# Memory of the split operands lent to raw weight tiles, and one float32 path for the first and last expert

## The chip, the cores and the metric

The kernel runs on one core of a Trainium2 chip. The metric is device time in microseconds of one execution. A core has a matrix engine (TensorE, PE in the profile, with its weight loads as PEld), a vector engine (DVE), a scalar engine (ACT), GpSimd (POOL) and SyncE (SP). Here SP issues nearly all transfers from device memory, in its program's order.

## The reference

Two layers of a transformer run over 256 latent tokens and 256 context tokens, 1024 features wide. Each layer has a modulated norm, a mixer of four groups (two convolutions, spatial gating, attention), an output projection, and a channel mixer: a dense SwiGLU in layer 0, and in layer 1 a top-2-of-8 expert SwiGLU, on the latent tokens alone. The last part matters here:

```python
logits = (xt @ router_w).astype(jnp.float32) + router_b.astype(jnp.float32)
top_val, top_idx = lax.top_k(logits, TOP_K)
gates = jax.nn.softmax(top_val, axis=-1)
...
def swiglu(h, w1, w3, w2):
    return (jax.nn.silu(h @ w1) * (h @ w3)) @ w2
```

Each expert has w1 and w3 of 1024 x 3584 and w2 of 3584 x 1024 in float32: 44 MB an expert, 352 MB in all, and every expert is read once. An expert computes only the tokens that chose it. A final norm closes.

## The kernel before

**Weight tiles.** All weights come as tiles of 128 partitions x 2048 float32 (1024 KB), in one fixed order, `plan`. `w_dma` (line 102 issues) takes a free slot, the one that has been free longest, and asks SP for the next tile, as long as a slot is free; `release` gives a slot back when the tile's last reader has been written into the program, and calls `w_dma` again. SP then waits at each issue until the engine that read the slot's old tile has finished. Slots in `kept` are not given back; the test is `o not in kept`, by equality. Most slots are pieces of one large buffer, `FA`; as the first layers end, regions of `FA` that hold nothing any more join the list, so that there are more slots at the end than at the start.

**Two ways to multiply.** In most stages a tile is *split*: by halves (chunks of 1024 columns), ACT copies a chunk to float32r as the high part (line 135), DVE subtracts for the low part (line 136), and PE makes three matmuls of each product (lines 243 to 245, `mm3`). High and low parts stand in a ring of slots in the buffer `RA`: four slots (`wbuf`, from column 9728), and a fifth at columns 4096 to 6143 that `w_more` adds when the experts begin. In the other way, *raw*, PE multiplies the tile as it came, in float32, with at most 64 tokens, two halves of the columns side by side on the array (line 1372 for w1 and w3, line 1395 for w2); nothing is split.

**Experts.** After the router the experts are ordered by token count into eight places. Place 0 is always expert 0. Places 1, 3 and 5 (`NAT`) take small experts and always run raw, with room for 64 tokens; places 2, 4 and 6 always run split, with room for 128. Places 0 and 7 have both programs under a branch on the count: split with more than 64 tokens, raw otherwise. Tokens beyond the room go through a loop at the end that is skipped when there are none. In the profiled execution both took the raw program: lines 1372 and 1395 ran 2240 and 560 matmul records, five places of 448 and 112.

A place has seven slices of the hidden width. `up_nat` or `up` multiplies w1 and w3 of a slice (two tiles each), then `lower` multiplies w2 of the slice before (two tiles), then `flip` turns the result: 42 tiles a place, 336 in all. Small steps are hung between the tiles by a list, `agenda`: the gates, `fetch` and `gather` (which pick and modulate the next place's tokens by one-hot matmuls: line 1289 for a raw place, lines 1301, 1306, 1307 and 1310 for a split one), and `scatter` (which adds a place's result to the tokens). While place 6 runs, both gathers for place 7 are hung in, since the branch is still open. Gathered tokens of split places stand in `RA` from column 0, turned slices from column 6144. The order is written out by hand: each engine runs its own part in the program's order.

**Around the first place.** Layer 1's mixer ends with the output projection `w_out` (its four tiles are split). Then come the residual, the router's logits (from slices of `xT`, in `FA` at `oT + 3072`), the ranks, and at line 1579 the load of expert 0's token count, which every engine waits for before it branches; SP too. Transfers of expert tiles begin before that, as slots come free.

Of the kernel before, what the change touches and what calls it, by code (L numbers as in the profile page):

```python
# [34 lines left out]
def tile_hybrid_headgroup_dit_moe(ctx: ExitStack, tc: tile.TileContext, a, out: bass.AP):  # L35
# [8 lines left out]
    RA = cp.tile([P, 17920], F32R, name="RA")  # L44
# [17 lines left out]
    def ra(o, *shape):  # L62
        n = 1
        for s in shape:
            n *= s
        v = RA[:, o:o + n]
        if len(shape) == 2:
            v = v.rearrange("p (a b) -> p a b", a=shape[0])
        return v
# [15 lines left out]
    NW = [4]  # L85
    LESS = [3]
    LIM = [None]
    wbuf = [(ra(W_O + i * 2048, 1024), ra(W_O + i * 2048 + 1024, 1024)) for i in range(4)]
# [22 lines left out]
    kept = []  # L111

# [5 lines left out]
    def w_split(n):  # L118
        while st["split"] < min(n, len(chunks) if LIM[0] is None else LIM[0]):
# [12 lines left out]
            if i >= len(wbuf):  # L132
                wbuf.append(wbuf[i - NW[0]])
            wh, wl = wbuf[i]
# [688 lines left out]
    NAT = (1, 3, 5)  # L823
    RANK = (0, 7, 1, 6, 2, 5, 3, 4)
# [22 lines left out]
    for j, entry in enumerate(plan):  # L847
        if entry[0][0] in ("modr", "mod") or entry[0][0].startswith("moe") and entry[0][1] in NAT:
# [7 lines left out]
    LIM[0] = first_chunk(0)  # L856
    ring = wbuf[0:4]
# [253 lines left out]
    free_slots.append(fa(oM1, 2048))  # L1111

# [5 lines left out]
    HG, HT = 0, 6144  # L1118
# [40 lines left out]
    free_slots.append(fa(oT + 3072, 2048))  # L1159
    for t in range(2):  # L1160
# [113 lines left out]
    gsb = cp.tile([P, NE], F32, name="gsb")  # L1274


    hns = [ybuf[0].rearrange("p (a b) -> p a b", a=8)] + [fa(4096, 8, 64)] * (NE - 1)
    sn = [fa(4096 + 512 + i * 256, 256) for i in range(2)]
# [3 lines left out]
    def gather(e, o, nat=False):  # L1282
        if nat:
            hn = hns[e]
# [8 lines left out]
        h = hg[e] = H(ra(HG + e % 2 * 2048, 8, P), ra(HG + e % 2 * 2048 + 1024, 8, P))  # L1293
# [20 lines left out]
    def slots(e, o_, gcol):  # L1314
# [5 lines left out]
        v = ra(HS + 1024 + (e % 2) * 256, 256)  # L1320
        nc.scalar.copy(v, b[:, 0:256])
        g = gsb[:, e:e + 1]
# [20 lines left out]
    def raw_tile(key):  # L1343
        if key[1] in (0, NE - 1):
            i = st["use"]
            assert i == st["split"]
            j = chunks[i][0]
            for c in range(2):
                if i + c >= len(wbuf):
                    wbuf.append(wbuf[i + c - NW[0]])  # L1350
            st["use"] = st["split"] = i + 2
        else:
            j = raw_j.pop(0)
# [9 lines left out]
    def up_nat(p, i):  # L1363
        b1, b3 = bank(), bank()
        hn = hns[p]
        for w, b in (("moe_w1", b1), ("moe_w3", b3)):
            for r in range(2):
                j, raw = raw_tile((w, p, i))
                for q in range(4):
                    k = 4 * r + q  # L1370
                    for c in range(2):
                        nc.tensor.matmul(b[64 * c:64 * c + 64, 0:256], hn[:, k], raw[:, q, 256 * c:256 * c + 256],  # L1372
                                         start=k == 0, stop=k == 7, skip_group_check=True)
# [3 lines left out]
            if w == "moe_w1":  # L1377
                s = sn[i % 2]
                nc.scalar.activation(s, b1[:, 0:256], AF.Silu)
        nc.vector.tensor_mul(s, s, b3[:, 0:256])  # L1380
        return s

    def flip_nat(g, s):
        b = bank()
        for j in range(2):
            nc.tensor.transpose(b[:, j * P:j * P + P], s[:, j * P:j * P + P], ident)  # L1386
        nc.scalar.copy(hidn[g % 2], b[:, 0:256])  # L1387
        return hidn[g % 2]

    def down_nat(p, i, hid, ya):  # L1390
# [387 lines left out]
```

## Time and profile before

| | |
|---|---|
| median of 3 runs | 1655.82 us (1655.27 to 1655.94) |
| the profiled execution's own time | 1655.85 us |
| its span, first to last instruction | 1654.0 us |
| mean granted TensorE clock | 0.978 |
| PE busy | 1572.3 us, 95% |
| DVE, ACT busy | 935.2 us (57%), 727.8 us (44%) |
| read from device memory | 489.36 MB |

The page gives each engine's busy time over the span and in 40 slices of 41.35 us, the clock the array was granted, and how busy the 16 DMA engines were. Matmul records overlap and their ends are modelled, so that PE's busy share hides short waits: the time that a stretch of known work takes is a better measure than the busy time in it. A table of stretches names for each its bounds and length, then each engine's busy time with the count of instructions, the granted clock, the DMA share and the rate. Everything from about 787 us to 1637 us is the eight expert places.

### The profile page before, as it was taken

Reading aid. Unit: us, or ns where it says so; the run is one execution under the profiler, and the core shown is the slowest. Engines: PE = TensorE matmul, PEld = TensorE weight load, DVE = VectorE, ACT = ScalarE, POOL = GpSimd, SP = SyncE. Lnnn points to the kernel's source line nnn. Section 1 sums busy time; section 2 is a strip of 40 time slices with the busy share of each in tenths; the row PEclk is TensorE's granted clock in tenths of the full one; section 3 lists DMA queues with packets and bytes.
Section 4 is the critical chain, followed back from the end, with each engine's and each line's share of the span. In section 5 each row is a group of like instructions: output and inputs, shape, how many; then the busy total and the mean of one; then the engine's idle time right before and its main releaser. Section 6 shows DMA issues by size and latency. Waiting matters only on the chain. (4 is left out here: it accounts for less than half of the span.)

```text
span 1654.0 us, 23342 instructions
## 1 busy us (share of the span) xinstructions
PE 1572.3 (95%) x8970; PEld 1164.0 (70%) x8970; DVE 935.2 (57%) x1597; ACT 727.8 (44%) x1101; POOL 25.9 (2%) x54
## 2 busy tenths in 40 slices
PE   7999999999999999999998889999999999999995
PEld 5787788888888797887554447875578855678652
DVE  3794578976465799745101038861188811788301
ACT  4447556222224564564211137761277711677201
POOL 0100000000000001000000000000000000000001
PEclk8999899999999999998999999999999999999998
DMA  8635233756584545524899999999999999999895
GB/s 344 234 144 190 107 110 124 271 211 249 180 304 136 187 167 195 187 84 174 359 421 421 421 421 419 422 381 403 421 421 420 377 392 420 421 420 361 333 421 226
DMA packets 69236, 492.14 MB, mean 298 GB/s; under 512 B 7985, under 2 KB 8753, under 8 KB 9713
## 3 DMA queue, kind: packets, MB, share of 16 engines
q1 hardware_dynamic: 67856, 486.97, 74.9%
q0 software_dynamic: 816, 2.72, 0.6%
q8 instruction: 77, 1.26, 0.3%
q10 hardware_dynamic: 432, 0.74, 0.1%
q14 instruction: 55, 0.44, 0.1%
HBM read 489.36 MB, written 1.05 MB: 296 GB/s over the span
## 5 line engine op out<-in xcount | busy, mean ns | idle before, releaser
L136 DVE TENSOR_TENSOR RA<-FA,RA 128x1024 fp32r<-128x1024 f32 x404 | 486.8, 1227 | 151.8 <-ACT RA L135 148.7
L135 ACT CAST RA<-FA 128x1024 fp32r<-128x1024 f32 x404 | 417.5, 1051 | 248.7 <-PE mm L245 146.8
L243 PE MATMUL mm<-RA 128*128 128x512 f32 (+1 forms) x976 | 371.5, 381 | 10.5 <-ACT RA L135 4.4
L244 PE MATMUL mm<-RA 128*128 128x512 f32 (+1 forms) x976 | 365.7, 375 | 3.8 <-DVE RA L136 2.3
L245 PE MATMUL mm<-RA 128*128 128x512 f32 (+1 forms) x976 | 365.0, 374 | 0.0
L243 PEld LDWEIGHTS mm<-RA 128*128 128x128 f32 x976 | 186.0, 191 | 50.0 <-issue 5.8
L1372 PE MATMUL mm<-FA 128*64 128x256 f32 x1792 | 209.4, 385 | 9.2 <-DMA FA<-in_moe_w_dram 7.9
L243 PE MATMUL acc<-RA 128*128 128x512 f32 (+1 forms) x552 | 207.8, 377 | 4.9 <-DVE RA L765 1.8
L244 PEld LDWEIGHTS mm<-RA 128*128 128x128 f32 x976 | 186.4, 191 | 36.1 <-DVE RA L136 3.2
L245 PEld LDWEIGHTS mm<-RA 128*128 128x128 f32 x976 | 186.1, 191 | 32.7
L245 PE MATMUL acc<-RA 128*128 128x512 f32 (+1 forms) x552 | 204.3, 370 | 0.0
L244 PE MATMUL acc<-RA 128*128 128x512 f32 (+1 forms) x552 | 204.2, 370 | 0.0
L1372 PEld LDWEIGHTS mm<-FA 128*64 128x64 f32 x1792 | 126.3, 138 | 79.6 <-issue 12.2
L1395 PE MATMUL acc<-FA 128*64 128x512 f32 x560 | 132.2, 598 | 7.6 <-DMA FA<-in_moe_w_dram 6.3
L243 PEld LDWEIGHTS acc<-RA 128*128 128x128 f32 x552 | 104.5, 189 | 26.2 <-issue 3.4
L245 PEld LDWEIGHTS acc<-RA 128*128 128x128 f32 x552 | 104.4, 189 | 17.9 <-issue 0.3
L244 PEld LDWEIGHTS acc<-RA 128*128 128x128 f32 x552 | 104.5, 189 | 16.2 <-issue 0.2
L1380 DVE TENSOR_TENSOR FA<-FA,mm 128x256 f32<-128x256 f32 x35 | 14.7, 421 | 159.8 <-PE mm L1372 159.8
L310 DVE SCALAR_TENSOR_TENSOR FA<-FA 128x1024 f32<-128x1024 f32 x80 | 94.4, 1221 | 6.5 <-DMA FA<-in_w_modt_dram 6.4
L1395 PEld LDWEIGHTS acc<-FA 128*64 128x64 f32 x560 | 37.5, 136 | 70.2 <-issue 54.4
L1310 DVE TENSOR_TENSOR RA<-lc,RA 128x128 fp32r<-128x128 f32 x32 | 9.3, 290 | 127.1 <-ACT RA L1307 127.1
L1387 ACT COPY FA<-mm 128x256 f32<-128x256 f32 x35 | 13.0, 372 | 142.4 <-PE mm L1386 142.4
(270 smaller groups left out, 1252.8 us busy)
## 6 DMA issues: line engine op xcount, KB each, us to landing
FA<-in_moe_w_dram SPq DMA_DIRECT2D x336, 1024.0 KB, 15.0
FA<-in_w_modt_dram SPq DMA_DIRECT2D x28, 1024.0 KB, 4.9
FA<-in_ffn_dram SPq DMA_DIRECT2D x22, 1024.0 KB, 5.0
FA<-in_ffn_w_dram SPq DMA_DIRECT2D x22, 1024.0 KB, 4.9
FA<-in_w_mod_dram SPq DMA_DIRECT2D x20, 1024.0 KB, 7.0
FA<-in_w_in_dram SPq DMA_DIRECT2D x20, 1024.0 KB, 5.1
FA<-in_w_out_dram SPq DMA_DIRECT2D x12, 1024.0 KB, 4.9
FA<-in_x_dram SPq DMA_DIRECT2D x2, 1024.0 KB, 8.3
```

What stands on the lines that cost most here:

```text
L135: nc.scalar.copy(wh, raw)
L136: nc.vector.tensor_sub(wl, raw, wh)
L243: nc.tensor.matmul(ps, ll, rh, start=start, stop=False, skip_group_check=True)
L244: nc.tensor.matmul(ps, lh, rl, start=False, stop=False, skip_group_check=True)
L245: nc.tensor.matmul(ps, lh, rh, start=False, stop=stop, skip_group_check=True)
L310: nc.vector.scalar_tensor_tensor(o, raw[:, c], 1.0, csb[:, s], op0=OP.mult, op1=OP.mult, accum_out=modT[l][:, 2 * r + c, s:s + 1])
L1310: nc.vector.tensor_sub(h.l[:, k], v["h32"], h.h[:, k])
L1372: nc.tensor.matmul(b[64 * c:64 * c + 64, 0:256], hn[:, k], raw[:, q, 256 * c:256 * c + 256], start=k == 0, stop=k == 7, skip_group_check=True)
L1380: nc.vector.tensor_mul(s, s, b3[:, 0:256])
L1387: nc.scalar.copy(hidn[g % 2], b[:, 0:256])
L1395: nc.tensor.matmul(ya[64 * hf:64 * hf + 64, :], hid[:, jj * P + 64 * r:jj * P + 64 * r + 64], raw[:, 2 * hf + jj], start=i == 0 and r == 0 ...
```

## The change

- `RA` is no longer one buffer but seven (`piece`, R0 to R6), cut at columns 0, 4096, 8192, 9728, 11776, 13824 and 15872. R3 to R6 are the four ring slots. The same memory can be declared again, as float32 for raw tiles or as float32r.
- R1 becomes two more slots for raw tiles, from the time when the last product that reads it (`v`) is written into the program until the end. The fifth ring slot, which lay there, is gone: the ring has four slots throughout.
- `lend` gives pieces out as slots that are used once each. R3 to R6 and R0 (six tiles) are lent when `w_out` has been written; R3 to R6 (four tiles) again in the first slice of places 3 and 5, and before place 7. `take_back` declares them as float32r again: R0 after place 0, R3 to R6 at the end of places 1, 3 and 5.
- `release` tests `kept` by identity, and a call of `w_dma` follows at once where a region of `FA` is added at `oT + 3072`.
- Places 0 and 7 run raw whatever the count. With more than 64 tokens the branch runs each tile's matmuls twice, for two halves of the tokens, with the same weights; with 64 or fewer, the program is the raw one as before. The split gather for place 7 is gone from place 6, and the raw one is spread over place 6 as over the others (`GATH`).
- The gathered tokens of split places have one place in R0 instead of two (only even places use it), and the buffers of the last norm lie elsewhere in `FA`.

```diff
-    RA = cp.tile([P, 17920], F32R, name="RA")
+    def piece(i, dt=F32R):
+        return cp.tile([P, RW[i]], dt, name=f"R{i}", tag=f"R{i}", bufs=1)
+    RO, RW = (0, 4096, 8192, 9728, 11776, 13824, 15872), (4096, 4096, 1536, 2048, 2048, 2048, 2048)
+    RA = [piece(i) for i in range(7)]
...
-    NW = [4]
+    NW = 4
...
     def release(j):
         o = raw_of.pop(j)
-        if o not in kept:
+        if not any(o is x for x in kept):
             free_slots.append(o)
         w_dma()
...
+    def lend(*pieces):
+        for i in pieces:
+            RA[i] = piece(i, F32)
+            for o in range(0, RW[i], 2048):
+                t = RA[i][:, o:o + 2048]
+                lent.append(t)
+                kept.append(t)
+                free_slots.append(t)
+        w_dma()
+
+    def take_back(*pieces):
+        for t in lent:
+            assert not any(t is x for x in list(raw_of.values()) + free_slots)
+        for i in pieces:
+            RA[i] = piece(i)
...
-    def w_more(wh, wl):
-        assert st["split"] >= NW[0] and len(wbuf) == st["split"]
-        wbuf.append((wh, wl))
-        NW[0] += 1
...
-        w_split(i + NW[0] - less - LESS[0])
+        w_split(i + NW - less - LESS[0])
...
     NAT = (1, 3, 5)
+    TWO = (0, NE - 1)
+    RAW = NAT + TWO
...
     for t in range(2):
         nc.scalar.copy(vc[:, t], accs[2 + t])
+    RA[1] = piece(1, F32)
+    free_slots += [RA[1][:, 0:2048], RA[1][:, 2048:4096]]
+    w_dma()
...
     accs = w_out(1, (1, 2, 0, 3), yn1, mid)
     free_slots.append(fa(oM1, 2048))
+    lend(3, 4, 5, 6, 0)
...
     free_slots.append(fa(oT + 3072, 2048))
+    w_dma()
...
+                    for n, hn in enumerate((hns[p], hn_2)[0:1 + two]):
+                        for c in range(2):
+                            nc.tensor.matmul(b[64 * c:64 * c + 64, 256 * n:256 * n + 256], hn[:, k],
+                                             raw[:, q, 256 * c:256 * c + 256], start=k + n == 0, stop=k == 7,
+                                             skip_group_check=True)
...
-    w_more(ra(4096, 1024), ra(5120, 1024))
...
+    def body(g, nat, two=False):
         e, i = divmod(g, NSL)
+        s = up_nat(e, i, two) if nat else up(e, i, hg[e], moe_next)
         if g and g - 1 in hts:
+            lower(g - 1, nat if i else e - 1 in RAW, two)
+            if i == 0 and 1 < e < NE - 1 and nat:
+                lend(3, 4, 5, 6)
+        hts[g] = flip_nat(g, s, two) if nat else flip(g, s)
...
+    either(first_n, first_place)
+    take_back(0)
...
-            if e < NE - 2:
-                plan_late(fetch(e + 1, e + 1 in NAT), GATH)
-            else:
-                plan_late(fetch(e + 1, False), [0] + [9 + 4 * k + d for k in range(KD) for d in (0, 1, 1)])
-                plan_late(fetch(e + 1, True), [45] + [49 + 4 * k + d for k in range(KD) for d in (0, 1, 1)])
+            plan_late(fetch(e + 1, e + 1 in RAW), GATH)
         body(g, e in NAT)
         if e in NAT and i == NSL - 1:
-            w_split(st["use"] + NW[0])
+            take_back(3, 4, 5, 6)
+            w_split(st["use"] + NW)
...
+    lend(3, 4, 5, 6)
+    fg, xg, sq, ss = fa(oM1 + 4096, D), fa(oM1 + 6144, 2, D), fa(oM2 + 3584, 2, D), sm(4)
...
+    either(last_n, last_place)
+    take_back(3, 4, 5, 6)
```

`either` loads the count, writes the program with two halves under the branch's true side and the one with a single half under the other, and asserts that both leave the same lists.

On SP the issues before the first count is loaded stand as follows; `in_moe_w_dram` are expert tiles, FA and R the buffers they land in. Before:

```order
69 L102 DMA FA<-in_w_out_dram 128x2048 x2
70 L102 DMA FA<-in_moe_w_dram 128x2048
71 L102 DMA FA<-in_w_out_dram 128x2048 x2
72 L102 DMA FA<-in_moe_w_dram 128x2048 x8
73 L1579 TENSOR_LOAD ti
```

And with the change (R_5326 is R1, R_5756 to R_5759 are R3 to R6, R_5760 is R0):

```order
70 L108 DMA FA<-in_moe_w_dram 128x2048
71 L108 DMA FA<-in_w_out_dram 128x2048 x2
72 L108 DMA FA<-in_moe_w_dram 128x2048 x2
73 L108 DMA R_5326<-in_moe_w_dram 128x2048 x2
74 L108 DMA FA<-in_moe_w_dram 128x2048 x8
75 L108 DMA R_5756<-in_moe_w_dram 128x2048
76 L108 DMA R_5757<-in_moe_w_dram 128x2048
77 L108 DMA R_5758<-in_moe_w_dram 128x2048
78 L108 DMA R_5759<-in_moe_w_dram 128x2048
79 L108 DMA R_5760<-in_moe_w_dram 128x2048 x2
80 L108 DMA FA<-in_moe_w_dram 128x2048
81 L1603 TENSOR_LOAD ti
```

Nine expert tiles stood ahead of the load of the count, and twenty stand there now. Before, two more followed behind the branch before the first one that needs a tile of place 0 to be used up.

On ACT, in place 6, the split gather (lines 1306 and 1307, once for each of eight blocks of features) stood among the copies of the split. Before:

```order
702 L135 CAST RA<-FA 128x1024 x4
703 L1306 ACTIVATE lc<-mm,modT_75 128x128
704 L1307 ACTIVATE RA<-mm,modT_75 128x128
705 L1442 CAST RA<-mm 128x512
706 L135 CAST RA<-FA 128x1024 x3
707 L1306 ACTIVATE lc<-mm,modT_75 128x128
708 L1307 ACTIVATE RA<-mm,modT_75 128x128
```

With the change the same stretch of place 6 holds the copies (line 159 now, each to one of four ring slots), the raw gather (line 1318), and nothing of a split gather:

```order
829 L159 CAST R_10439<-FA 128x1024
830 L159 CAST R_10436<-R_5326 128x1024
831 L159 CAST R_10437<-R_5326 128x1024
832 L159 CAST R_10438<-R_5326 128x1024
833 L1318 ACTIVATE FA<-mm,modT_81 128x64
834 L1470 CAST R_7311<-mm 128x512
```

The sixteen activations of the split gather, its matmuls on PE and its subtractions on DVE are gone from place 6; some of the copies read their tile from R1.

More of the change, by code (lines that the diff above doesn't have):

```diff
@@ L65, in ra @@
             n *= s
[L66 removed]
+        i = max(i for i in range(7) if RO[i] <= o)
+        assert o + n <= RO[i] + RW[i]
+        v = RA[i][:, o - RO[i]:o - RO[i] + n]
         if len(shape) == 2:
@@ L1312, in gather, with slots @@
         return steps
-    def slots(e, o_, gcol):
+    def slots(e, o_, gcol, part=0):
         b = bank()
@@ L1343, in raw_tile @@
     def raw_tile(key):
[L1344 to L1351, printed above, removed]
-        else:
-            j = raw_j.pop(0)
+        j = raw_j.pop(0)
         assert plan[j][0] == key
@@ L1509, in tile_hybrid_headgroup_dit_moe, with lower @@
     ya = {}
-    def lower(g, nat):
+    def lower(g, nat, two=False):
         e1, i1 = divmod(g, NSL)
         if i1 == 0:
-            ya[e1] = bank("acc") if nat else [bank("acc") for _ in range(2)]
+            ya[e1] = [bank("acc") for _ in range(1 + two if nat else 2)]
         if nat:
@@ L1519, in lower @@
         if i1 == 4:
-            sl[0] = slots(e1, one_hot(e1), list(place(e1))[1])
+            gc = list(place(e1))[1]
+            sl[:] = [slots(e1, one_hot(e1), gc)] + ([slots(e1, oh_2, gc, 1)] if two else [])
         if i1 == NSL - 1 and 0 < e1 < NE - 2:
@@ L1557, in scat_now, with first_place @@
         del agenda[:]
-    def first_place(nat):
-        assert st["use"] == st["split"] == LIM[0] == first_chunk(0)
-        LIM[0] = first_chunk(2)
-        if not nat:
-            first = fetch(0, False)
-            first[0]()
-            w_split(st["use"] + NW[0])
-            hbuf.extend([ybuf[i][:, j * P:j * P + P] for i in range(2) for j in range(2)])
-            run(first[1:])
-            del hbuf[2:]
+    def first_place(two):
+        if two:
+            run(fetch(0, True, 1))
         plan_late(gates(), range(2, 22))
@@ L1571, in first_place @@
         for i in range(NSL):
-            body(i, nat)
-        lower(NSL - 1, nat)
+            body(i, True, two)
+        lower(NSL - 1, True, two)
         for fs in agenda:
@@ L1615, in ends, with last_place @@
         nc.gpsimd.tensor_tensor(xg[:, t, c], xs[:, 2 + t, c], fg[:, c], op=OP.mult)
[L1617 to L1618 removed]
+    def last_place(two):
         scat(NE - 2, False)
[L1620 to L1623 removed]
+        if two:
+            run(fetch(NE - 1, True, 1))
         for i in range(NSL):
[L1625 to L1626 removed]
+            body((NE - 1) * NSL + i, True, two)
+        lower(LAST, True, two)
         nc.gpsimd.dma_start(fg, a["final_g"].to_broadcast([P, D]))
[L1628 to L1637 removed]
+        scat_now(NE - 1, [lambda t=t, hf=hf: ends(t, hf) for hf in range(2) for t in range(2)])
+    either(last_n, last_place)
+    take_back(3, 4, 5, 6)
     raws = [fa(oR, 2048), fa(oR + 2048, 2048)]
@@ L1656, in nxt @@
             raw = raws[(n // 2) % 2][:, c * 1024:c * 1024 + 1024]
-            wh, wl = ring[n % 4]
+            wh, wl = [ra(W_O + n % 4 * 2048 + k * 1024, 1024) for k in range(2)]
             nc.scalar.copy(wh, raw)
```

164 lines of the change are left out of this document (72 added, 92 removed).

## Prediction

> **What bounds the kernel now.** I read the page's slices first, to find the stretch that the change touches.
>
> ```profile
> PE   7999999999999999999998889999999999999995
> DVE  3794578976465799745101038861188811788301
> DMA  8635233756584545524899999999999999999895
> ```
>
> From slice 19 (787 us) on DMA is at 9 nearly throughout: the expert weights. DVE tells the ways apart: near 0 in raw places, 8 in split ones. PE's 9 cannot be trusted for short waits, since matmul ends are modelled. So I cut the trace into stretches of known work:
>
> ```profile
> core 0: us, PE busy (x) PEld busy (x) DVE busy (x) ACT busy (x) POOL busy (x), PEclk, DMA share, GB/s
> 786.70:866.00 79.30, 78.61 (x588) 44.40 (x588) 9.11 (x42) 13.65 (x28) 0.00 (x0) 0.98 0.96 394
> 892.20:973.60 81.40, 71.50 (x494) 36.57 (x490) 4.73 (x14) 10.08 (x26) 0.00 (x0) 1.00 1.01 421
> 973.60:996.20 22.60, 18.24 (x77) 12.21 (x75) 15.05 (x15) 13.14 (x15) 0.00 (x0) 0.92 1.01 421
> 996.20:1104.70 108.50, 108.50 (x501) 88.04 (x498) 95.69 (x91) 83.29 (x93) 0.00 (x0) 1.00 1.01 409
> 1121.60:1192.30 70.70, 70.70 (x502) 37.05 (x498) 9.44 (x21) 11.04 (x28) 0.00 (x0) 1.00 1.01 417
> 1192.30:1212.70 20.40, 18.18 (x77) 12.18 (x75) 14.88 (x15) 13.16 (x15) 0.00 (x0) 0.92 1.01 421
> 1408.90:1429.50 20.60, 16.64 (x74) 10.96 (x75) 15.09 (x16) 13.25 (x16) 0.00 (x0) 1.00 1.02 422
> 1429.50:1549.40 119.90, 118.10 (x557) 96.05 (x555) 99.46 (x102) 88.43 (x109) 0.00 (x0) 1.00 0.97 384
> 1549.40:1611.40 62.00, 61.31 (x466) 34.35 (x467) 7.51 (x14) 5.12 (x13) 0.00 (x0) 1.00 0.96 393
> 1611.40:1636.90 25.50, 20.70 (x122) 8.55 (x122) 0.98 (x3) 1.46 (x4) 0.55 (x1) 1.00 0.83 344
> ```
>
> In order: place 0; most of place 1; the passage into split place 2; its body; place 3, the same stretch as place 1's; the passage into 4; into 6; 6's body up to place 7; place 7 in two parts. Places 1 and 3 do the same products, as the line's own stretches show:
>
> ```profile
> 892.20:973.60 81.40, 42.16 (x354) 24.95 (x350) 1.00 1.01 421
> 1121.60:1192.30 70.70, 41.04 (x354) 23.95 (x350) 1.00 1.01 417
> ```
>
> Line 1372 ran 354 matmuls in both, with the array's clock at 1.00, but place 1 took 10.7 us longer, with DMA at its full 421 GB/s: place 1 waits for its weights, place 3 does not. At that rate a tile of 1024 KB takes 2.49 us. Place 3's stretch uses 354/16 + 12 = 34 tiles, one in 2.08 us, faster than they come; a split body uses 36 in 108.5 us, one in 3.01 us, slower. So the store of loaded tiles grows in split places and shrinks in raw ones, and the first two places are both raw. They start from too little:
>
> ```profile
> L102 SPq DMA_DIRECT2D FA<-in_moe_w_dram x11: 327/328/739, 683.2 to 777.9; - x11
> 786.75 5.52 PE L1372 MATMUL mm<-FA,lc 128*64 128x256 f32 x36 [2.43 <-issue]
> 740.00:760.00 20.00, 20.00 (x128) 15.60 (x127) 12.46 (x43) 11.80 (x23) 0.00 (x0) 1.00 0.71 256
> 760.00:780.00 20.00, 17.96 (x109) 16.50 (x108) 12.08 (x45) 7.73 (x16) 0.59 (x16) 0.81 0.10 28
> ```
>
> Eleven expert tiles have been asked for when place 0's first matmul runs at 786.75. The slots are full, and DMA stands at 0.10 from 760 to 780. The waits on SP say the same:
>
> ```profile
> SPq L102 <- PE mm L1372: 158.8, 91, 11.4
> SPq L1579 <- DVE pv L1493: 19.8, 1, 19.8
> ```
>
> Issues wait for PE to free a slot, and for 19.8 us SP sits at the count with nothing it could have issued.
>
> **The change part by part.** *More tiles at the start.* SP's order has 20 expert tiles ahead of the first use, against 11. The nine: two in R1, one FA slot that the test by identity gives back (before, an equal view in `kept` dropped it), six lent. Do they arrive in time? R1 waits for `v`, whose last matmul ran at 714; R3 to R6 and R0 wait for `w_out`:
>
> ```profile
> L245 PE MATMUL acc<-RA x35: 279/389/498, 713.7 to 765.0; 128*128 128x512 f32 x32, 128*128 128x256 f32 x3
> ```
>
> From 765 to 787 DMA can move 22/2.49 = 8 tiles, more than the seven left. From the first release (a tile is 16 records, of which 36 took 5.52 us) near 790 the stream then runs without a pause. The 62 further tiles up to the last one of place 1's stretch take 62 x 2.49 = 154 us, and the first needs the time of an idle queue:
>
> ```profile
> FA<-in_w_out_dram SPq DMA_DIRECT2D x12, 1024.0 KB, 4.9
> ```
>
> They land by 790 + 154 + 5 = 949. PE needs that one about 12 us before the 973.6 at which it is done now, near 960. So there is a margin of some 11 us, four tiles, and place 1 takes place 3's pace: **10.7 us**. The last tiles of place 0 are late now too; the waits from 860 to 975 name PE's products of w2 as well:
>
> ```profile
> PE mm L1372 <- DMA FA<-in_moe_w_dram: 5.4, 11, 0.8
> PE acc L1395 <- DMA FA<-in_moe_w_dram: 4.6, 8, 1.4
> ```
>
> I take one such wait for place 0, an estimate: **1 us**.
>
> *Passages.* ACT's copies wait there for tiles:
>
> ```profile
> ACT RA L135 <- DMA FA<-in_moe_w_dram: 13.4, 10, 4.7
> ```
>
> PE idles 4.4, 2.2 and 4.0 us in the three passages (22.60 - 18.24, and so on), part of it for the turned slices, which stays. With tiles on chip early I take 3, 1 and 1.5 us: **5.5 us**, between 0 and 10.6.
>
> [...] The passages into 2 and 4 show a clock of 0.92, the one into 6 shows 1.00. [...]
>
> *Place 6 loses the split gather.*
>
> ```profile
> 996.20:1103.90 107.70, 57.78 (x144) 27.02 (x144) 1.00 1.01 411
> 1429.50:1541.00 111.50, 58.56 (x144) 27.07 (x144) 1.00 0.99 392
> 1429.50:1541.00 111.50, 4.24 (x28) 4.20 (x28) 1.00 0.99 392
> ```
>
> The same 144 matmuls of line 243 take 107.7 us in place 2 and 111.5 in place 6; the third row is line 1301 there, absent from place 2. Gain **3.8 us**.
>
> *Place 7.* Its first 32 tiles took 62.0 us, 1.94 each; the last ten 25.5. At 1.94 they take 19.4: **6.1 us**. The cover must grow by three tiles: three permanent slots and four lent ones make seven (17 us), and DMA has room to fill them, since place 6 leaves it at 384 GB/s because slots are full. Places 3 and 5 do not wait now, so their loans are worth nothing alone; they keep the store up when all starts earlier. Over one split and one raw place DMA needs 84 x 2.49 = 209 us and PE 108.5 + 70.7 + 20.4 + 17 (the rest of the raw place, 1104.7 to 1121.6) = 217, so the stream holds.
>
> *A ring of four for five.* This is the cost.
>
> ```profile
> L136 DVE TENSOR_TENSOR RA<-FA,RA 128x1024 fp32r<-128x1024 f32 x258 | 306.9, 1222 | 64.8 <-ACT RA L135 61.9
> L135 ACT CAST RA<-FA 128x1024 fp32r<-128x1024 f32 x258 | 265.2, 1051 | 72.7 <-PE mm L245 36.4 <-PE acc L245 20.7 <-DMA FA<-in_moe_w_dram 13.4
> L243 PE MATMUL mm<-RA 128*128 128x512 f32 x336 | 137.3, 409 | 4.4 <-ACT RA L135 4.4
> L1443 DVE TENSOR_TENSOR RA<-mm,RA 128x512 fp32r<-128x512 f32 x21 | 14.5, 690 | 7.7 <-ACT RA L1442 6.7
> L1432 ACT ACTIVATE lc<-mm 128x512 f32<-128x512 f32 x21 | 12.6, 598 | 5.7 <-PE mm L245 5.6
> ```
>
> ACT waits 57 us for PE to free a ring slot, PE 4.4 us for ACT: the ring is full nearly always. A chunk needs 1.05 + 1.22 = 2.27 us to be split, PE uses one in 107.7/72 = 1.50 us. With four slots, three chunks lie ahead when one is freed, 4.5 us of work against 2.27 and one other operation of ACT or DVE (0.6 to 0.7 us, as in the last two rows). The margin is 1.5 us; only two or three extra operations on top of each other pass it. I take 1 us in all. A bound from above: if each of the 21 split slices lost one 0.7 us operation, 15 us; from below, 0.
>
> *At nothing:* the two-halves branch, since both counts took the other side; declaring pieces again, which issues nothing. The last norm's buffers: its weights load into a slot whose last tile comes just before the final ten, about 19 us ahead of the end, so that these ten hide the load; without that cover it would cost at most its own time:
>
> ```profile
> FA<-in_final_g_dram POOLq DMA_DIRECT2D x1, 512.0 KB, 8.5
> ```
>
> *Sum.* 10.7 + 1 + 5.5 + 3.8 + 6.1 - 1 = 26.1 us. The profiled execution took 1655.85 us (span 1654.0 and 1.85 around it), the median 1655.82, so it stands for the runs. 1655.85 - 26.1 = 1629.7, and since the passages may add the clock and the gather also leaves ACT and DVE, I say **1629 us**.
>
> **Rivals.**
>
> *Half the gain is lost* (the ring costs its 15 us, or lent pieces come late). If no loan helps at all, three permanent slots (7.5 us of stream) remain: place 1 gains 7.5 for 10.7, and 6.1 + 3.8 stay, 17 us in all: 1639. With the ring's 15 us off the full sum it is 1645. Against the late loans: the row of `w_out` ends at 765. For it: the ring's margin is worked out from means.
>
> *The ring of four starves PE: slower.* In places 2, 4 and 6 each freed slot sets ACT, DVE and PE going one after the other. If hand-overs and other work bring that loop over 4 x 1.50 = 6.0 us, it sets the pace; at 7 us a chunk takes 1.75, and 252 chunks lose 63 us: 1629 + 63 = 1692. It turns the whole slower from 6.4 us on (0.107 us for each of 252 chunks, 27 us). Against it: the loop is 2.27 us of splitting, at most 1.50 of matmuls and the hand-overs, under 5.
>
> *The stream stays the bound: same.* If the tiles that come earlier only fill the store earlier, and the whole is set by bytes, nothing is won. Against it: from 790 the 316 remaining tiles need 316 x 2.49 = 787 us, to 1577, and now the last one lands at about 1635. The floor of the stream lies 58 us lower. It would need a rate of 316 x 1.049 MB / 845 us = 392 GB/s to bind as now, and the trace holds 421 for whole places.
>
> [...]
>
> **How the numbers follow.** Prefetch covers place 1 and the end: 0.70, 1621 to 1637 (passages and clock 5 to 8 us better, ring 7 us worse). Half lost, 1637 to 1651: 0.17. Better than 1621: 0.04. Same: 0.04. Ring starves, slower: 0.05. Within 0.2% (3.3 us) a measurement of this kernel cannot tell from no change; faster 0.91, same 0.04, slower 0.05. The range 1618 to 1645 leaves out the last two, the worst of the half, and the little below.
>
> **What would show it.** Right: 20 expert tiles asked for before the first raw matmul; place 1's 34 tiles in about 71 us; no wait of the raw products for DMA in places 1 and 7; a split body of 108 us in all three split places, place 6 no longer apart. Wrong: split bodies above 110 us with PE waiting for line 159 or 160 (the ring); R3 to R6 issued after 787, or SP held at one of them while FA slots are free; DMA under 421 GB/s while PE waits for it.

## The result and the profile after

The changed kernel takes 1626.29 us (median of 4 runs, 1622.73 to 1628.01), the kernel before 1655.55 us beside it (4 runs, 1651.65 to 1655.94). The ratio is 0.983, with a 95% interval of 0.980 to 0.985: some 1.7% less time. The forecast was 1629 us, with 1618 to 1645 as its range.

The profiled execution took 1626.18 us and its span is 1624.4 us, against 1655.85 and 1654.0. The DMA slices of its page:

```profile
DMA  9635323766674545547799999999999999999993
```

DMA's 9s start as they did, but the last slice has a 3: the last weights are there well before the end. The table of stretches of the changed kernel, cut at the same steps of the program as the prediction's table (columns as there):

```profile
core 0: us, PE busy (x) PEld busy (x) DVE busy (x) ACT busy (x) POOL busy (x), PEclk, DMA share, GB/s
786.90:866.10 79.20, 78.69 (x586) 44.54 (x588) 9.12 (x42) 13.67 (x28) 0.00 (x0) 0.98 0.91 369
892.10:959.60 67.50, 67.50 (x495) 36.35 (x492) 4.74 (x14) 10.10 (x26) 0.00 (x0) 1.00 1.01 421
959.60:978.30 18.70, 16.47 (x75) 10.96 (x75) 13.80 (x14) 12.25 (x14) 0.00 (x0) 1.00 1.01 420
978.30:1086.40 108.10, 108.10 (x499) 87.84 (x497) 95.30 (x91) 83.31 (x93) 0.00 (x0) 1.00 1.01 421
1103.30:1174.50 71.20, 71.20 (x507) 37.38 (x504) 9.44 (x21) 11.06 (x28) 0.00 (x0) 1.00 1.01 421
1389.40:1408.10 18.70, 16.47 (x75) 10.96 (x75) 13.71 (x14) 12.27 (x14) 0.00 (x0) 1.00 1.01 422
1408.10:1516.20 108.10, 108.10 (x499) 87.85 (x497) 95.32 (x91) 83.31 (x93) 0.00 (x0) 1.00 1.00 401
1516.20:1525.20 9.00, 6.17 (x29) 4.64 (x27) 3.67 (x4) 1.53 (x2) 0.00 (x0) 1.00 0.98 368
1525.20:1587.20 62.00, 61.46 (x468) 34.60 (x470) 6.94 (x13) 5.12 (x13) 0.55 (x1) 1.00 1.01 420
1587.20:1606.50 19.30, 18.78 (x122) 8.60 (x118) 0.97 (x3) 1.46 (x4) 0.00 (x0) 1.00 0.49 202
1606.50:1624.40 17.90, 1.41 (x10) 0.78 (x8) 6.71 (x20) 4.32 (x10) 4.94 (x4) 0.59 0.16 63
```

In order: place 0; place 1; the passage into place 2; its body; place 3; the passage into 6; the body of place 6; the step into place 7; place 7 in two parts; the end. Each answers to a row of before (the passage into place 4, not shown, takes 18.7 us too):

| stretch | before, us | after, us | gain | predicted |
|---|---|---|---|---|
| place 0 | 79.3 | 79.2 | 0.1 | 1 |
| place 1 | 81.4 | 67.5 | 13.9 | 10.7 |
| passages into 2, 4 and 6 | 22.6, 20.4, 20.6 | 18.7, 18.7, 18.7 | 7.5 | 5.5 |
| body of place 2 | 108.5 | 108.1 | 0.4 | } -1 (ring) |
| place 6 with the step into 7 | 119.9 | 117.1 | 2.8 | } 3.8 (gather) |
| place 7 | 87.5 | 81.3 | 6.2 | 6.1 |
| the end | 17.1 | 17.9 | -0.8 | 0 |
| sum | | | 30.1 | 26.1 |

The spans differ by 29.6; the rest lies in stretches that are not in the table (place 3 takes 71.2 us for 70.7, for example). The lead at the start shows in the issues up to 787 us, by the buffer they land in:

```profile
L108 SPq DMA_DIRECT2D FA<-in_moe_w_dram x12: 327/328/328, 683.6 to 772.6; - x12
L108 SPq DMA_DIRECT2D R<-in_moe_w_dram x8: 328/382/435, 715.1 to 766.6; - x8
```

The first raw product, from the timeline, comes after them all:

```profile
786.88 7.14 PE L1393 MATMUL mm<-FA,lc 128*64 128x256 f32 x48 [1.76 <-issue]
```

Twenty expert tiles are asked for, 8 of them into pieces of the old `RA`, before the first product at 786.88. The waits for expert tiles from 866 us to the end, first before, then with the change:

```profile
ACT RA L135 <- DMA FA<-in_moe_w_dram: 13.4, 10, 4.7
PE mm L1372 <- DMA FA<-in_moe_w_dram: 7.9, 14, 1.3
PE acc L1395 <- DMA FA<-in_moe_w_dram: 6.3, 12, 1.4
```

```profile
ACT R L159 <- DMA FA<-in_moe_w_dram: 1.7, 2, 1.2
```

PE's matmuls wait for none any more, and 0.5 us of ACT's 1.7 lie in the passage into place 2.

### The profile page after: what moved, and what is told of

The parts are those of the page before. It is cut to its first block, busy times and chain, and to the rows that moved or that the text cites. A ratio compares the mean times of both kernels' runs of the same rounds, so it can differ in the third digit from the quotient of the medians.

```text
span 1624.4 us, 23225 instructions
## 1 busy us (share of the span) xinstructions
PE 1562.1 (96%) x8938; PEld 1162.2 (72%) x8938; DVE 932.9 (57%) x1587; ACT 723.1 (45%) x1085; POOL 25.9 (2%) x54
## 5 line engine op out<-in xcount | busy, mean ns | idle before, releaser
L160 DVE TENSOR_TENSOR R<-FA,R 128x1024 fp32r<-128x1024 f32 x368 | 443.9, 1227 | 130.9 <-ACT R L159 127.7
L159 ACT CAST R<-FA 128x1024 fp32r<-128x1024 f32 x368 | 381.4, 1051 | 229.5 <-PE mm L264 131.4
L262 PE MATMUL mm<-R,R 128*128 128x512 f32 (+1 forms) x976 | 369.9, 380 | 10.0 <-ACT R L159 4.4
L263 PE MATMUL mm<-R,R 128*128 128x512 f32 (+1 forms) x976 | 364.7, 374 | 3.5 <-DVE R L160 2.3
L264 PE MATMUL mm<-R,R 128*128 128x512 f32 (+1 forms) x976 | 363.6, 373 | 0.0
L262 PEld LDWEIGHTS mm<-R,R 128*128 128x128 f32 x976 | 185.4, 190 | 48.7 <-ACT R L159 5.1
L262 PE MATMUL acc<-R,R 128*128 128x512 f32 (+1 forms) x552 | 208.2, 378 | 4.9 <-DVE R L784 1.8
L263 PEld LDWEIGHTS mm<-R,R 128*128 128x128 f32 x976 | 185.8, 190 | 35.7 <-DVE R L160 3.2
L264 PEld LDWEIGHTS mm<-R,R 128*128 128x128 f32 x976 | 185.7, 190 | 32.3
L263 PE MATMUL acc<-R,R 128*128 128x512 f32 (+1 forms) x552 | 204.6, 371 | 0.0
L264 PE MATMUL acc<-R,R 128*128 128x512 f32 (+1 forms) x552 | 204.5, 371 | 0.0
L1393 PE MATMUL mm<-FA 128*64 128x256 f32 x1488 | 174.5, 387 | 2.3 <-issue 1.4
L1393 PEld LDWEIGHTS mm<-FA 128*64 128x64 f32 x1488 | 104.8, 138 | 59.5 <-issue 10.4
L262 PEld LDWEIGHTS acc<-R,R 128*128 128x128 f32 x552 | 104.7, 190 | 26.3 <-issue 3.4
L264 PEld LDWEIGHTS acc<-R,R 128*128 128x128 f32 x552 | 104.5, 189 | 17.9 <-issue 0.3
L263 PEld LDWEIGHTS acc<-R,R 128*128 128x128 f32 x552 | 104.7, 190 | 16.5 <-issue 0.3
L1423 PE MATMUL acc<-FA 128*64 128x512 f32 x416 | 96.9, 596 | 1.0 <-ACT FA L1414 1.0
L495 DVE SCALAR_TENSOR_TENSOR FA<-FA,pv 128x512 f32<-128x512 f32 (+1 forms) x128 | 74.1, 612 | 1.2 <-ACT FA L491 0.7
```

Source lines behind the costliest of these rows:

```text
L159: nc.scalar.copy(wh, raw)
L160: nc.vector.tensor_sub(wl, raw, wh)
L262: nc.tensor.matmul(ps, ll, rh, start=start, stop=False, skip_group_check=True)
L263: nc.tensor.matmul(ps, lh, rl, start=False, stop=False, skip_group_check=True)
L264: nc.tensor.matmul(ps, lh, rh, start=False, stop=stop, skip_group_check=True)
L495: nc.vector.scalar_tensor_tensor(acc, src, w, acc, op0=OP.mult, op1=OP.add)
```

## Experiments

Where a few microseconds count, one more number is used beside the medians: the time from the first raw product to the end of the span in the profiled run. What the engines compute before that product is the same in all kernels but one (the transfers ahead of it differ), and yet the product came at anything from 781.70 to 788.94 us (more on this at the end). This time has a spread of its own: the changed kernel's two profiled runs differ by 2.1 us in it.

| kernel | median, us (runs) | ratio to before, 95% | first raw product to end, us |
|---|---|---|---|
| before | 1654.85 to 1655.93 (beside each group) | | 867.3 |
| changed | 1626.29 (4) | 0.9826 [0.9804, 0.9848] | 837.5 |
| changed, again | 1625.51 (5) | 0.9822 [0.9807, 0.9837] | 839.6 |
| no loan at the start | 1637.19 (4) | 0.9881 [0.9865, 0.9898] | 853.7 |
| no later loans | 1625.11 (4) | 0.9812 [0.9796, 0.9828] | 838.7 |
| before, ring of four | 1654.84 (10) | 0.9991 [0.9982, 1.0001] | 871.7 |
| before, one gather | 1653.16 (8) | 0.9980 [0.9967, 0.9994] | 864.8 |
| ring of three | 1639.40 (4) | 0.9919 [0.9896, 0.9943] | 851.8 |
| one slot less | 1628.41 (4) | 0.9849 [0.9828, 0.9871] | 840.4 |
| dense at the scatter | 1626.16 (4) | 0.9830 [0.9807, 0.9854] | 838.4 |
| dense there and in the router | 1627.30 (4) | 0.9841 [0.9819, 0.9862] | 838.6 |
| dense, lent twice | 1625.65 (5) | 0.9816 [0.9797, 0.9835] | 837.4 |
| that, and dense ahead of place 7 | 1630.13 (4) | 0.9849 [0.9833, 0.9865] | 844.1 |

**The loan at the start left out.**

```diff
-    lend(3, 4, 5, 6, 0)
+    w_dma()
```

> The changed kernel without the loan of six tiles (R3 to R6, R0) at the end of the mixer; the later loans and the 14 permanent slots stay. 14 expert tiles instead of 20 are asked for before the first raw matmul. Theory of the lead: in the changed kernel the stream runs without a pause from the first release to the passage into place 2, and the two tiles used there (numbers 88 and 89) are taken the moment they land; so each tile missing at the start costs its 2.49 us, six cost 15 us, and the time is about 1641 us (1638 to 1643). Rival, that the permanent slots carry the gain and the loan only filled slack: place 1 ends with some 4 us of slack in the changed kernel, and no more than 5 us come back, 1627 to 1631.

1637.19 us: 10.9 more than the changed kernel, between the two expectations and nearer to the first. Place 1 and the passage behind it, in this kernel:

```profile
890.60:965.10 74.50, 69.34 (x495) 36.29 (x492) 4.73 (x14) 10.08 (x26) 0.00 (x0) 1.00 1.01 421
965.10:988.10 23.00, 18.22 (x79) 12.25 (x80) 14.63 (x15) 13.44 (x16) 0.00 (x0) 0.97 1.01 421
```

Place 1 takes 74.5 us for 67.5, with the same 495 matmuls, and the passage 23.0 for 18.7. That is the lead at work: six tiles fewer, and the raw places wait again. (The profiled run is the slowest of the four; the medians differ by about what these two stretches show, 7.0 and 4.3 us.) Why 11 us and not the 15 of six tiles? The stretches of place 0, first of the changed kernel, then of this one, show it:

```profile
787.00:800.00 13.00, 12.49 (x98) 8.13 (x100) 2.47 (x13) 4.81 (x6) 0.00 (x0) 0.87 0.63 231
820.00:830.00 10.00, 10.00 (x78) 5.75 (x76) 0.42 (x1) 1.19 (x3) 0.00 (x0) 1.00 0.69 277
```

```profile
787.00:800.00 13.00, 12.48 (x106) 8.28 (x104) 2.47 (x13) 5.96 (x9) 0.00 (x0) 0.92 0.76 299
820.00:830.00 10.00, 10.00 (x72) 5.19 (x70) 0.42 (x1) 1.19 (x3) 0.00 (x0) 1.00 1.01 419
```

From 820 to 830 us the changed kernel's stream runs at 277 GB/s for 419: at 421 GB/s this is 3.4 us given back, of 15. (The 231 for 299 up to 800 us is mostly a matter of when the runs start: this one's first raw product came 1.6 us earlier, and in the same 13 us after it the rate is 248.) The landings in the two traces agree: counted from the first raw product, tile 88, which the passage into place 2 needs, lands at 184.0 us in the changed kernel and at 195.2 here, 11.2 us later and not 15. The loans are used once; when they are spent, the tiles again wait for a permanent slot. (That this pause is a lack of slots is shown below, where the pieces are lent twice.)

**The later loans left out** (the two calls of `lend(3, 4, 5, 6)` behind place 1).

> The changed kernel without the loans in places 3 and 5 and before place 7 (12 tiles in all); the loan at the start stays. Theory of the lead: the three permanent slots are 7.5 us of stream and cover the 6.1 us that place 7 was short; 0 to 2 us lost, 1626 to 1628. Rival, that place 7 lives on the loan: its last ten tiles wait for DMA again, and 5 to 6 us come back, 1631 to 1632.

1625.11 us: they are worth nothing that can be measured. The prediction had said so of those in places 3 and 5; it had counted on the four before place 7, and they too are not needed.

**The kernel before with the ring of four alone.**

```diff
-    w_more(ra(4096, 1024), ra(5120, 1024))
```

> The kernel before with a ring of four slots of split operands instead of five in the expert places; nothing else is changed. Theory: three chunks ahead (4.5 us of PE work) are enough against 2.27 us of splitting and one other operation, so 0 to 1 us, 1655.5 to 1656.5, with split bodies of 108 us. Rival, the ring starves PE: each of 21 split slices loses one operation of 0.7 us, 15 us, 1670, with split bodies of 113 us or more.

The ratio is 0.9991 [0.9982, 1.0001] (the profiled run was the slowest of the ten, hence its 871.7 in the table). The split bodies of places 2, 4 and 6 take 108.5, 108.5 and 111.7 us, for 108.5, 108.5 and 111.5 with five slots. The fifth slot cost nothing to give up.

**The kernel before with a single gather for place 7.** The split gather is moved from place 6 into the split program of place 7, which is not taken here.

> The kernel before with the split gather for place 7 moved out of place 6 and under the branch that is not taken; slots and ring as before. Theory: place 6's body becomes that of places 2 and 4, 108 us for 112, and 3.8 us are won, 1651.7. Rival: place 7 is short of tiles at its end anyway, and a place 6 that ends earlier gives the stream less time to run ahead, so the gain goes into longer waits in place 7 and the time stays at 1655.5.

The median is 2.8 us lower, the interval gives 1.0 to 5.5. The trace shows both theories half right. Body of place 6, the step into place 7, and place 7 in two parts, in this kernel:

```profile
1430.30:1538.40 108.10, 108.10 (x500) 87.94 (x499) 95.14 (x92) 83.32 (x94) 0.00 (x0) 1.00 1.00 410
1538.40:1548.60 10.20, 6.74 (x33) 5.09 (x31) 2.86 (x4) 0.87 (x2) 0.00 (x0) 1.00 0.61 222
1548.60:1610.60 62.00, 61.48 (x454) 34.60 (x456) 6.91 (x12) 5.12 (x13) 0.00 (x0) 0.97 0.95 386
1610.60:1636.90 26.30, 21.98 (x136) 9.27 (x132) 1.00 (x3) 1.46 (x4) 0.55 (x1) 1.00 0.85 352
```

The body takes 108.1 us for the 111.5 of before, as in the changed kernel, and the passage ahead of it 19.1 for 20.6. Then the step into place 7 takes 10.2 for 8.4 and place 7 itself 88.3 for 87.5. The last product ends at 1636.9 in both, but this run's first raw product came at 788.94 us and that of before at 786.75, so that from there the run is 2.2 us ahead, near the 2.8 of the medians. What was lost again lies at the branch, where PE waits 2.06 us for 0.43 (more on this below), and in place 7. The last tile lands at 1634.9 in both, just as the last product needs it, so place 7 still waits for its weights, as the rival had it; but its clock is lower too (0.97 for 1.00), and how much goes to which one trace cannot tell.

**A ring of three** (from the first place on).

```diff
-    NW = 4
+    NW = [4]
...
+    NW[0] = 3
```

> The ring of split operands has three slots instead of four from the first expert on; the fourth stays unused except when it is lent. My account of the ring: when a slot is freed with four slots three chunks lie ahead (4.5 us of matmuls) and splitting takes 2.27 us, so four slots have slack and cost nothing. With three, two chunks (3.0 us) lie ahead of a split of 2.27 us, some 0.4 us of hand-over between the engines, and any one other operation of ACT or DVE (0.6 to 0.7 us) that comes between: the slack is 0.3 us and most slices lose part of such an operation. Expected: split bodies of 110 to 116 us instead of 108.1, so 1632 to 1650. The rival, that PE's pace hides any ring because its matmuls are queued ahead, expects 1625 to 1628 and bodies of 108. The prediction's rival of a starving ring, moved by one slot (a loop of 6 to 7 us over three slots), expects bodies of 150 us or more and 1750.

1639.40 us, 13 more: as the margin said. (The expectation's 0.4 us of hand-over were an estimate; in the changed kernel's body of place 2 DVE starts 0.04 us after the end of the copy that it waits for, at 988.33 us for 988.29.) The passage into place 6 and its body, in this kernel:

```profile
1390.10:1411.60 21.50, 19.27 (x78) 12.82 (x79) 12.99 (x14) 12.08 (x15) 0.00 (x0) 0.92 1.01 421
1411.60:1521.90 110.30, 109.67 (x495) 86.36 (x493) 96.26 (x91) 83.04 (x94) 0.00 (x0) 1.00 0.98 389
```

The body takes 110.3 us for 108.1, the passage 21.5 for 18.7, some of it by the clock (0.92). Place 4 lies between (109.3 and 19.9). With place 2 (108.5 and 20.9) the split places and their passages lose 10.0 us against the changed kernel's first profiled run. Another 2.6 are lost at the step into place 7 (11.6 for 9.0; PE's wait behind the branch is 4.98 us) and 1.7 in place 7 (82.9 for 81.3, its clock 0.97 from 1533.5 to 1596.0 us). The size of the whole agrees with the expectation, its place only in part: I had put all of it into the bodies (110 to 116). The starving ring (1750) is ruled out even for three slots. So the step from five slots to four costs nothing and that from four to three 13 us, of which 10 are seen in the split places.

**One permanent slot less** (the test in `release` drops one `FA` slot again).

> The changed kernel with one permanent slot of the large buffer dropped, as the test by equality dropped it before: 19 tiles instead of 20 ahead of the first use, and 13 permanent slots instead of 14. Taking six early tiles away cost 11 us, 1.8 us a tile. Theory (each tile of the start's lead is worth its share of stream, as far as the margin of 4.3 us at the end of place 1 is used up): the first two tiles lost are covered by the margin, so one tile costs 0 to 1 us: 1626 to 1627.5. Rival (every tile counts alike): 1628 to 1629.

1628.41 us, 2 to 3 more than the changed kernel's two medians. The intervals overlap; the trace decides. Place 1 and the passage into place 2 in this kernel:

```profile
885.40:953.00 67.60, 67.60 (x497) 36.36 (x494) 4.74 (x14) 10.11 (x26) 0.00 (x0) 1.00 1.01 421
953.00:974.00 21.00, 18.12 (x74) 12.07 (x74) 14.02 (x14) 12.29 (x14) 0.00 (x0) 0.92 1.01 420
```

And the longest wait for a weight tile there, from the waits:

```profile
ACT R L159 <- DMA R<-in_moe_w_dram: 3.4, 1, 3.4
```

Place 1 stays at 67.6: its margin was there, as the theory had it. But the passage behind it takes 21.0 for 18.7, with ACT 3.4 us late for a tile and the clock at 0.92. In the changed kernel ACT waits 0.5 us there: the lead is just used up at the second slice of place 2. So a tile less costs about a tile.

**Dense matmuls where the clock falls.** At the end of place 0, PE waits 2.2 us for the scatter's operands, and the granted clock is then 0.60 from 876.8 to 884.0 us. Nine matmuls of ones by ones, into the bank that the scatter's first product overwrites, fill this wait (n is 9 there, and 0 everywhere else):

```diff
                 def product(...):
                     w[0] = bank()
+                    warm(n, w[0])
```

> The changed kernel with nine more matmuls of 128 columns, whose results are thrown away, on PE where it waits 2.2 us at the end of place 0 for the scatter's operands. After that wait the granted clock falls to 0.50 for about 7 us. Theory (the wait lets the clock fall, and filling it keeps the clock): 877 to 884 runs at 1.00, 2 to 3.5 us gained, 1623 to 1624. Rival (the fall comes from something else, or the weights bind at once): no gain, or 0.5 us lost, 1626 to 1627.

Two stretches from there, of the changed kernel and then of this one:

```profile
870.70:874.00 3.30, 1.85 (x10) 0.40 (x6) 0.76 (x1) 0.59 (x1) 0.00 (x0) 1.00 1.01 420
...
876.80:884.00 7.20, 7.14 (x40) 4.18 (x42) 1.60 (x5) 0.39 (x1) 0.00 (x0) 0.60 1.01 419
```

```profile
870.70:874.00 3.30, 3.30 (x23) 2.01 (x20) 0.95 (x2) 0.59 (x1) 0.00 (x0) 1.00 0.99 407
...
876.80:884.00 7.20, 6.75 (x63) 4.48 (x64) 1.39 (x4) 0.38 (x1) 0.00 (x0) 1.00 1.02 424
```

The theory holds at this place: a clock of 1.00 for 0.60, and 63 matmuls for 40 in the same 7.2 us. Place 2's first split product comes 2.4 us earlier after the first raw one (172.1 us for 174.5). Yet the median is 1626.16, no gain. The trace shows tile 88 landing just as ACT asks for it in the passage into place 2 (ACT waits 0.5 us for a tile there), and I took the stream for what gave the gain back.

**The same in the router's stage.** Three such matmuls ahead of each group of the router's transposes, and five ahead of the rank product.

> As the run before, and in the router's stage too: three such matmuls ahead of each of the four groups of transposes, five ahead of the rank matmul. There the clock is 0.50 from 770 to about 791 us, while the matmuls have 8 columns or are few. Theory (a denser array keeps the clock): the gather at 778 to 785 us takes 3.5 us instead of 7, place 0's first products gain 1.5 to 2, the logits 1; the added matmuls cost up to 2 us on PE: 1.5 to 4 us less than the run before, 1619 to 1622. Rival (the dense matmuls are too few to hold the clock, or the wait for the count absorbs the gain): 0 to 2 us slower than the run before.

1627.30 us, no gain: the rival. The stretch of the gather ahead of place 0, in the changed kernel and then in this one:

```profile
778.20:785.10 6.90, 6.90 (x33) 6.73 (x32) 0.68 (x4) 2.83 (x7) 0.25 (x8) 0.50 0.52 209
```

```profile
778.60:782.30 3.70, 3.70 (x34) 3.59 (x33) 0.85 (x5) 2.80 (x7) 0.60 (x16) 1.00 0.71 288
```

And this kernel's first raw product, with the wait ahead of it, from the timeline:

```profile
786.28 7.25 PE L1395 MATMUL mm<-FA,lc 128*64 128x256 f32 x48 [3.95 <-issue]
```

The gather runs at a clock of 1.00 for 0.50 and takes 3.7 us instead of 6.9. PE then waits 3.95 us instead of 1.76, and the first product comes at 786.28 instead of 786.88. The trace has what it waits for: PE's own branch on the count, which lasts 4.37 us here and 3.81 in the changed kernel. It starts while matmuls written before it are still running, 2.3 us before their end in the changed kernel and only 0.7 here. So what the faster gather wins, the branch takes.

**The pieces lent twice.** With the dense matmuls at the scatter, and the six pieces handed out again in place 0 as soon as their tiles are used, four of them again in place 1:

```diff
             body(i, True, two)
+            if i == 2:
+                again(0, 3)
+            if i == 3:
+                again(3, 6)
...
-            if i == 0 and 1 < e < NE - 1 and nat:
+            if i == 0 and 0 < e < NE - 1 and nat:
```

> The dense matmuls at the end of place 0, and the six lent pieces handed out a second time within place 0 (for tiles 33 to 35 and 39 to 41), four of them once more in place 1. The dense matmuls alone won 2.4 us by the clock and gave 1.6 back at the passage into place 2, where tile 88 came late. In the changed kernel DMA pauses for some 3 us between 820 and 830, when the single-use loans are spent. Theory (the stream at tile 88 is the next bound, and the pause is a lack of slots): DMA at full rate from 800 to 890, tile 88 lands 3 us earlier against the first product, and the 2.4 us stay: 1623 to 1624.5, and 2 to 2.4 us less from the first raw product to the place-2 body. Rival (the loss at the passage is not the weights): nothing gained, 1626.

From 820 to 830 us DMA now moves 424 GB/s for 277:

```profile
820.00:830.00 10.00, 10.00 (x76) 5.55 (x74) 0.42 (x1) 1.19 (x3) 0.00 (x0) 1.00 1.02 424
```

So the pause was a lack of slots. Tile 88 lands 3 us earlier against the first product, and no expert tile is waited for in place 1 and the passage behind it. But the median is 1625.65, beside 1625.51 of the changed kernel in the same group: my theory of the stream as the next bound falls. The passage into place 2 tells what it is. Two stretches of it, with the clock, and PE's waits there, in this kernel:

```profile
959.60:962.40 2.80, 2.42 (x7) 1.94 (x8) 2.80 (x4) 2.32 (x4) 0.00 (x0) 0.69 1.01 421
962.40:964.40 2.00, 2.00 (x6) 1.56 (x6) 2.00 (x4) 0.64 (x2) 0.00 (x0) 0.59 0.99 414
```

```profile
PE mm L266 <- ACT R L163: 1.5, 1, 1.5
PE mm L267 <- DVE R L164: 0.8, 1, 0.8
```

And the same two views of the changed kernel:

```profile
962.20:965.00 2.80, 2.32 (x10) 1.94 (x11) 2.80 (x4) 2.80 (x4) 0.00 (x0) 1.00 1.01 421
965.00:967.00 2.00, 2.00 (x11) 1.65 (x10) 2.00 (x4) 1.34 (x3) 0.00 (x0) 1.00 1.00 418
```

```profile
PE mm L262 <- ACT R L159: 1.5, 1, 1.5
PE mm L263 <- DVE R L160: 0.8, 1, 0.8
```

PE waits the same 1.5 and 0.8 us in both. In the one the clock falls to 0.69 and 0.59 for some 4 us, in the other it stays at 1.00. From the first split product of place 2 to the first raw one of place 3 this kernel takes 127.0 us and the changed kernel 125.4: of the 2.2 us won up to that split product 1.7 are gone. Another 0.9 goes from place 6's first split product to place 7's first raw one (134.9 for 134.0), which holds the branch. The run with the dense matmuls alone has the same fall at this place (0.66 and 0.63).

**Dense matmuls ahead of the branch into place 7** (six, behind place 6, on top of the last).

> As the run before, and six more matmuls of 128 columns (1.4 us at full clock) at the end of place 6, ahead of the branch into place 7. PE waits there 1.4 to 2.6 us for its next instruction, and where it waits the longer time the clock falls to 0.50 for 4 us. Theory (the wait starts at the branch and runs beside matmuls already queued): the wait is covered in part, the clock stays, 0 to 2 us less than the run before. Rival (the branch is only reached when the queued matmuls are done): 1.4 us more than the run before, less what the clock gains.

1630.13 us, 4.5 more than the run before: worse than the rival said. PE's wait behind the branch and the branch itself on PE's sequencer, in this kernel and in the run before:

```profile
PE mm L1397 <- issue: 3.7, 1, 3.7
L1614 PEldq COMPARE_BRANCH  x1: 5919/5919/5919, 1521.2 to 1521.2; - x1
```

```profile
PE mm L1397 <- issue: 2.3, 1, 2.3
L1614 PEldq COMPARE_BRANCH  x1: 5939/5939/5939, 1519.0 to 1519.0; - x1
```

The added matmuls took 1.5 us, and the wait did not shrink but grew. The branch lasts the same 5.9 us in both, and as the theory had it, it runs beside matmuls already queued. But here 2.4 us of them were left when it started (the last one ends at 1523.6), and 3.8 in the run before (1522.8): the 1.4 us by which the wait grew. Why the six matmuls left less beside the branch and not more is not shown. Behind the longer wait the clock then stood at 0.50 from 1526 to 1532 us.

**The changed kernel again.**

> The changed kernel itself, unaltered, beside the two runs before: the measure for their differences of 1 to 2 us. 1625 to 1627.

1625.51 us, as expected. In its profiled run the wait at the branch into place 7 is 2.4 us where the first profiled run had 1.4, and there the clock falls to 0.50, where it had stayed at 1.00 in the first. The program is the same; PE's branch lasts 6.08 us here and 5.08 in the first run, 1.0 us longer, as the wait is.

The clock behind it in this run, from the stretches:

```profile
1525.00:1527.00 2.00, 2.00 (x12) 1.47 (x10) 0.00 (x0) 0.00 (x0) 0.00 (x0) 0.50 1.04 430
```

No version beat the changed kernel by more than its runs differ. Leaving out the later loans is as fast and simpler.

## Why the prediction was right

The forecast missed by 2.7 us of a gain of 29, and the likeliest case was the one that came. Some of the nearness is luck: place 1 and the passages came out 5.2 us better than their terms, place 0, the gather and the end 2.7 us worse. Step by step:

- *Place 1* (10.7 predicted, 13.9 found). The mechanism is shown by the loan left out: place 1 waits again. The size was read from place 3, and that yardstick was too long: its stretch holds the scatter of the split place before it, which place 1's does not. Two rows of the changed kernel's PE groups within place 3's stretch, which have no counterpart in place 1's:

```profile
L1504 PE MATMUL mm<-R 128*128 128x512 f32 x4 | 2.0, 500 | 0.0
L1505 PE MATMUL mm<-R 128*128 128x512 f32 x4 | 1.6, 396 | 0.0
```

  These 3.6 us are nearly the whole difference of 71.2 and 67.5. The 354 matmuls of one line were compared, not the stretch's other lines.
- *The margin of 11 us at the end of place 1* was mis-sized. It rested on a stream that runs "without a pause" from 790. It paused between 820 and 830, and the last tile of place 1's stretch landed at 953.5 us and not by 949; and with the shorter stretch PE needed it at 957.7 and not near 960. So the lead left there was 4.3 us, and at tile 88 none. That nothing was lost is luck of some half a microsecond, as the run with one slot less shows.
- *Place 0* (1 predicted, 0.1 found). The waits that I quoted lie in place 1: within place 0 PE waited 0.2 us for a tile, and its last products end within half a microsecond of each other in the two kernels.
- *Passages* (5.5 predicted, 7.5 found, bound 10.6). All three now take the same 18.7 us, and the clock in the first two is 1.00 for 0.92. PE's idle time, which I had priced, fell from 4.4, 2.2 and 4.0 us to 2.2 in each: 3.9 us and not 5.5, and none of it in the passage into place 4. The other 3.6 us are busy time of PE (18.24 and 18.18 to 16.47 in the first two), with the clock at 1.00 for 0.92. The sum has no term for that. What "the clock" is to add in the step to 1629 and in the chances was shown by no run; the runs showed these 3.6 us in its place, and they hid that the waits were priced too high.
- *The split gather gone* (3.8). The body of place 6 is now 108.1 like place 2's, and the kernel before with one gather shows the same 108.1. 1.0 us of it went again into PE's wait behind the branch into place 7 (1.45 us for 0.43), which I had not priced. That is the branch itself, 5.08 us for 4.00; as it was 6.08 in the changed kernel's other profiled run, nothing shows that this loss belongs to the change.
- *Place 7* (6.1 predicted, 6.2 found). Its last ten tiles take 19.3 us for 25.5, as said. Of the cover I named, the four lent tiles were not needed; nor was the loan at the start, since without it PE's matmuls wait for no tile in place 7 either. What the three permanent slots do alone was not run.
- *The ring* (-1, bounds 0 and 15): 0. The five-to-four step alone shows no cost; the margin of one slot that I worked out (1.5 us) agrees with the ring of three, where it is gone and 13 us are lost. The rival of half the gain lost was one slot away.
- *At nothing*: the branch in two halves, the re-declared pieces and the last norm's buffers show no cost in the experts. The end after the last product is 0.8 us longer; in all the profiled runs it takes 16.9 to 18.8 us, and in those of the kernel before and its variants 16.9 to 18.0, so this is not shown to be the change's.
- *The rivals*: the stream as the bound is refuted by the last weights' landing, well ahead of the end, and the starving ring by the ring of three. Half the gain lost would have needed a loan that comes late; the loan came in time.

## What to carry to other kernels

A stream that is slower than the work in one stage and faster in the next is worth its lead: count how many tiles are asked for before the first use, price each at the stream's time for one, and then look at each place where the store could run empty, not only at the one that waits now. A loan of idle memory used once gives back part of its lead as soon as it is spent (3.4 us of 15 here); look for the pause. And when a stretch is to be the yardstick of another, compare all the lines in both, not only the one that matters.

## What the runs showed of the hardware that was not expected

*The clock fell after short waits, and not each time.* Waits of 1.5 and 0.8 us close together left it at 1.00 in the changed kernel and took it to 0.59 and 0.63 in two others, at the same step of the same program. In the kernel before, the rows of the prediction say the same: PE idled 2.2 us in the passage into place 4 and the clock was 0.92, and 4.0 us in all in the passage into place 6 and the clock was 1.00. What decides whether such a wait lowers the clock, the runs do not show.

*A gain of 2 us can vanish without a new wait,* as the dense matmuls at the scatter show: the later waits were the same (1.5 and 0.8 us) and the clock behind them was not (0.66 and 0.63 for 1.00). And a program that is all but the same reaches place 0 at different times. First 100 us of the changed kernel's profiled run, and then of the run with one slot less, whose first product came 5.2 us earlier:

```profile
0.00:100.00 100.00, 90.25 (x521) 68.86 (x521) 64.35 (x123) 42.84 (x69) 9.31 (x16) 0.95 0.68 256
```

```profile
0.00:100.00 100.00, 89.82 (x540) 69.11 (x541) 66.61 (x126) 44.00 (x71) 9.30 (x16) 0.98 0.69 265
```

The clock is 0.95 in the one and 0.98 in the other. The runs of one kernel lie between 0.6 and 8.8 us apart here, and such differences ahead of the change can be a part of that; only the profiled runs tell the clock by stretches.

*A PE that looks busy can be at half clock.* Between 774 and 788 us the clock was 0.50 in both kernels, and PE was busy for 11.6 and 11.9 of these 14 us, with matmuls of 8 to 128 columns up to the first raw product. Denser matmuls ahead of it brought the gather to a clock of 1.00 for 0.50 (3.7 us for 6.9), which then won nothing, since a branch came next.

*A branch on a count held PE's sequencer for 3.8 to 6.1 us, and the matmuls queued ahead of it hid a part.* It started while matmuls written before it still ran. Into place 7 it lasted 4.00 us in the kernel before, 5.08 and 6.08 in two runs of the changed kernel, and 0.05 to 0.07 us on the other engines of the first two. PE's wait behind it, from 0.43 us in the kernel before to 4.98 in the ring of three, is what those matmuls do not cover: ahead of place 0 it was 1.76 us in the changed kernel, with 2.3 us of them left, and 3.95 with the dense matmuls in the router, with 0.7 left. Why the branch lasts so long on PE, and not always the same, the runs do not tell.
